# The last store of a row-wise softmax: one DMA of 16 rows per partition, or one of 8 rows and nine DMAs of unequal partition counts for the other 8

## The chip, the cores and the metric

The kernel runs on one core of one Trainium2 chip. The metric is device time in microseconds (us), lower is better. All input comes from the chip's DRAM and all output goes back there, 33.55 MB each way (the page: HBM read 33.55 MB, written 33.55 MB). The profile counts 16 DMA engines, and the semaphore of a store of all rows of a chunk was raised 16 times, here once by each. On the chip the kernel keeps the data in SBUF, in tiles of 128 partitions; a DMA moves rows between SBUF and DRAM. A DMA is issued by an engine's sequencer, and I call it landed when the last of these raises of its semaphore is on record: for the last store of the kernel before, issued at 144.77 us, the first of 16 came at 157.68 and the last at 158.86 us. The profile calls the compute engines DVE (VectorE), ACT (ScalarE), POOL and SP (which here only issues loads); "ACTq" is ACT's instruction sequencer, which issues the stores.

## The reference

```python
def reference(x):                       # x: 16 x 1024 x 512, float32
    x_max = np.max(x, axis=-1, keepdims=True)
    exp_x = np.exp(x - x_max)
    return (exp_x / np.sum(exp_x, axis=-1, keepdims=True)).astype(np.float32)
```

So there are 16384 rows of 512 numbers (2 KB); each row is loaded, normalized and stored once.

## The kernel before

The rows are cut into ten chunks. A chunk of R gives each of the 128 partitions R neighbouring rows, so that one partition's share of a store is one contiguous run of R x 2 KB. Chunks of 16 rows are computed in two groups of 8: DVE takes the maximum, ACT the exponential and the sum, DVE the reciprocal and the scaling. The last group is number 16, rows 8 to 15 of chunk 9. Each load and each store is a single DMA over all 128 partitions.

```python
CHUNKS = [
    (3, 0), (5, 3), (8, 8), (16, 16), (16, 32), (16, 48), (16, 64), (16, 80), (16, 0), (16, 16),
]
GROUP = 8
STORE_ROWS = {3: 8, 4: 8, 5: 8}        # chunks that are stored in two halves of 8 rows
# ... (cut)
        for a, b in zip(cuts, cuts[1:]):
            ends = b == R or b - since >= STORE_ROWS.get(k, R)
            groups.append((k, a, b, since if ends else None))
            since = b if ends else since
# ... (cut)
    def scale(g):
        k, a, b, since = groups[g]
        recip = stats.tile([P, b - a], F32, name="recip", tag="recip")
        nc.vector.reciprocal(out=recip, in_=sums[g])
        for r in range(a, b):
            nc.vector.tensor_scalar_mul(...)          # cut
        if since is not None:
            nc.scalar.dma_start(
                out=dst[k][:, since:b, :], in_=place[k][:, since:b, :]
            )
```

Of the kernel before, what the change touches and what calls it, by code (L numbers as in the profile page):

```python
# [1 line left out]

# [4 lines left out]

F32 = mybir.dt.float32
EXP = mybir.ActivationFunctionType.Exp
AX = mybir.AxisListType.X  # L10


CHUNKS = [
    (3, 0), (5, 3), (8, 8), (16, 16), (16, 32), (16, 48), (16, 64), (16, 80), (16, 0), (16, 16),
]
SBUF_ROWS = 96

EARLY = 8
AFTER_STORE = {2: [8], 3: [9]}

GROUP = 8

FINISH_BEFORE = (1, 2, 3)

STORE_ROWS = {3: 8, 4: 8, 5: 8}

ON_ACT = ()

AT_HEAD = {mybir.EngineType.SP: 1}



def loads_at_the_head(nc):

    main, body = nc.main_func.blocks[0], nc.main_func.blocks[1]
    for engine, count in AT_HEAD.items():
        loads = [
            i
            for i in body.instructions
            if i.engine == engine and type(i).__name__ == "InstDMACopy"  # L40
        ][:count]
        barrier = next(
            n
            for n, i in enumerate(main.instructions)
            if i.engine == engine and type(i).__name__ == "InstDrain"
        )
        for load in loads:
            body.instructions.remove(load)
        main.instructions[barrier:barrier] = loads


@with_exitstack
def kernel(
    ctx: ExitStack,
    tc: tile.TileContext,
    x: bass.AP,
    out: bass.AP,
):
    nc = tc.nc
    nc.at_finalize(loads_at_the_head)  # L60
    P = nc.NUM_PARTITIONS

    x_flat = x.flatten_outer_dims()
    out_flat = out.flatten_outer_dims()
    n, d = x_flat.shape
    assert n == P * sum(R for R, _ in CHUNKS)


    src, dst, at = [], [], 0
    for R, _ in CHUNKS:  # L70
        for flat, views in ((x_flat, src), (out_flat, dst)):
            part = flat[at : at + P * R, :]
            views.append(part.rearrange("(p r) d -> p r d", r=R))
        at += P * R

    data = ctx.enter_context(tc.tile_pool(name="data", bufs=1))
    stats = ctx.enter_context(tc.tile_pool(name="stats", bufs=4))
    held = data.tile([P, SBUF_ROWS, d], F32, name="held")
    place = [held[:, s : s + R, :] for R, s in CHUNKS]


    groups = []
    for k, (R, _) in enumerate(CHUNKS):
        m = max(1, round(R / GROUP))
        cuts = [R * i // m for i in range(m + 1)]
        since = 0
# [4 lines that stand above are left out]
    shift = [None] * len(groups)  # L91
    sums = [None] * len(groups)

    def load(k):
        queue = nc.scalar if k in ON_ACT else nc.sync
        queue.dma_start(out=place[k], in_=src[k])

    def rowmax(g):
        k, a, b, _ = groups[g]
        shift[g] = stats.tile([P, b - a], F32, name="shift", tag="shift")  # L100
        nc.vector.reduce_max(  # L101
            out=shift[g], in_=place[k][:, a:b, :], axis=AX, negate=True
        )

    def exps(g):
        k, a, b, _ = groups[g]
        sums[g] = stats.tile([P, b - a], F32, name="sums", tag="sums")
        for r in range(a, b):
            nc.scalar.activation(  # L109
                out=place[k][:, r, :],  # L110
                in_=place[k][:, r, :],
                func=EXP,
                bias=shift[g][:, r - a : r - a + 1],
                scale=1.0,
                accum_out=sums[g][:, r - a : r - a + 1],
# [7 lines that stand above are left out]
            nc.vector.tensor_scalar_mul(  # L123
                out=place[k][:, r, :],
                in0=place[k][:, r, :],
                scalar1=recip[:, r - a : r - a + 1],
            )
        if since is not None:
            nc.scalar.dma_start(
                out=dst[k][:, since:b, :], in_=place[k][:, since:b, :]  # L130
            )
        if b == CHUNKS[k][0]:
            for later in AFTER_STORE.get(k, ()):
                load(later)

    with tc.manual_schedule():
        for k in range(EARLY):
            load(k)
        waiting = None
        for g, (k, a, _, _) in enumerate(groups):  # L140
            if waiting is not None and a == 0 and k in FINISH_BEFORE:
                scale(waiting)
                waiting = None
            rowmax(g)
            exps(g)
            if waiting is not None:
                scale(waiting)
            waiting = g
        scale(waiting)


# [1 line left out]
_INS = ['x']  # L153
_OUTS = [((16, 1024, 512), 'float32')]


# [23 lines left out]
```

## Time and profile before

| | before |
|---|---|
| time, median of 2 | 162.55 us (162.31 to 162.79) |
| span of the profiled run (that run took 161.52 us) | 159.7 us |
| mean DMA rate over the span | 420 GB/s |
| last store issued, and landed | 144.77 us, 158.86 us |
| last data of the 16 DMA engines | between 157.33 and 158.52 us |

These are lines of the page of the kernel before: the busy time of DVE and ACT, then the busy tenths and the rate of the DMA engines in 40 slices of the span, and the DMA total.

```profile
DVE 123.9 (78%) x162; ACT 93.3 (58%) x257; POOL 0.2 (0%) x4
...
DMA  7999999899999999999999999999999999999993
GB/s 269 433 464 411 389 447 446 383 412 466 402 441 431 460 435 396 439 418 468 427 414 439 414 484 427 396 447 402 435 439 476 418 402 468 443 402 468 427 410 164
DMA packets 3315, 67.13 MB, mean 420 GB/s; under 512 B 368, under 2 KB 368, under 8 KB 624
```

Compute is not the limit: DVE is busy 78% and ACT 58% of the span. The DMA row stands at 9 (90% or more) from the second slice to the next to last. The timeline of the end shows how far compute is ahead. Columns: start, duration, engine, line, operation.

```profile
141.24 0.20 DVE L121 RECIPROCAL recip<-sums 128x8 f32<-128x8 f32 x1 [2.48 <-ACT held L109]
141.48 3.26 DVE L123 TENSOR_SCALAR held<-held,recip 128x512 f32<-128x512 f32 x8
144.77 0.34 ACTq L129 DMA_DIRECT2D out_dram<-held  x1
```

After 144.77 us no engine computes, and yet the kernel lasts 15 us more: the DMA engines work off a queue. The first packets of the store issued at 144.77 start at 147.65 us, when an engine is through with its part of the store ahead. The next lines cut that tail into windows. Columns: window; its length; busy us of DVE, ACT and POOL with instruction counts; granted clock; share of DMA engine time; GB/s. A packet is counted in the window where it starts, so a share can exceed 1.

```profile
150.00:153.00 3.00, 0.00 (x0) 0.00 (x0) 0.00 (x0) 1.00 1.14 492
153.00:156.00 3.00, 0.00 (x0) 0.00 (x0) 0.00 (x0) 1.00 0.83 360
156.00:159.00 3.00, 0.00 (x0) 0.00 (x0) 0.00 (x0) 1.00 0.48 208
159.00:162.00 3.00, 0.00 (x0) 0.00 (x0) 0.00 (x0) 1.00 0.00 0
```

Here share and rate fall together: 492/1.14, 360/0.83 and 208/0.48 are all about 432 GB/s. While a DMA engine is busy, it moves bytes at the same rate in all three windows. In the packet records, each 32 KB packet (one partition's share) of the last store takes 1.213 us (one took 1.226); the 128 packets form 16 rows of eight, back to back, one row for each engine. The engines end within 1.2 us of each other.

### The profile page before, as it was taken

The page shows a single profiled execution, that of the slowest core. Times are in us where ns is not written, and L with a number is a line of the kernel's source. Part 1 is how long each engine was busy: PE and PEld are TensorE (multiplying, and loading weights), DVE is VectorE, ACT ScalarE, POOL GpSimd, SP SyncE. Part 2 cuts the span into 40 slices and gives each one's busy share as a digit, 9 for nine tenths or more (in the row PEclk, how much of TensorE's full clock was granted, in tenths as well). Part 3 has the DMA queues.
Part 4 walks back from the last instruction along what each step waited for, and adds up shares of the span by engine and source line. Part 5 has one row for each costly group of instructions (what it writes and reads, how often), then busy time and mean ns, then how long its engine had stood idle before and what let it go on. Part 6 is the DMA issues. An engine that isn't in the chain of part 4 may idle for free.

```text
span 159.7 us, 521 instructions
## 1 busy us (share of the span) xinstructions
DVE 123.9 (78%) x162; ACT 93.3 (58%) x257; POOL 0.2 (0%) x4
## 2 busy tenths in 40 slices
DVE  0481870799699999999999999999999999762000
ACT  0718129208994959595868677686859595930000
POOL 0000000000000000000000000000000000000000
DMA  7999999899999999999999999999999999999993
GB/s 269 433 464 411 389 447 446 383 412 466 402 441 431 460 435 396 439 418 468 427 414 439 414 484 427 396 447 402 435 439 476 418 402 468 443 402 468 427 410 164
DMA packets 3315, 67.13 MB, mean 420 GB/s; under 512 B 368, under 2 KB 368, under 8 KB 624
## 3 DMA queue, kind: packets, MB, share of 16 engines
q1 hardware_dynamic: 1440, 33.56, 49.5%
q10 hardware_dynamic: 1872, 33.56, 48.9%
q14 instruction: 3, 0.02, 0.0%
HBM read 33.55 MB, written 33.55 MB: 420 GB/s over the span
## 4 chain that ended last, share of the span: by engine, by line
DVE 70%; ACT 14%; issue 3%; DMA 3%; DVEq 0%; ACTq 0%
DVE shift L101 38%; DVE held L123 30%; ACT held L109 14%; DMA held<-in_x_dram 3%; DVE recip L121 2%; DVEq L175 0%; ACTq L109 0%
## 5 line engine op out<-in xcount | busy, mean ns | idle before, releaser
L109 ACT ACTIVATE held<-held,shift 128x512 f32<-128x512 f32 x128 | 90.5, 709 | 43.4 <-DVE shift L101 33.2
L101 DVE TENSOR_REDUCE shift<-held 128x8 f32<-128x4096 f32 (+2 forms) x17 | 70.6, 4161 | 4.5 <-DMA held<-in_x_dram 4.5
L123 DVE TENSOR_SCALAR held<-held,recip 128x512 f32<-128x512 f32 x128 | 52.2, 481 | 0.6
L109 ACT ACTIVATION_READ_ACCUMULATOR held<-held,shift 128x1 f32 x128 | 24.0, 187 | 0.0
L121 DVE RECIPROCAL recip<-sums 128x8 f32<-128x8 f32 (+2 forms) x17 | 3.3, 193 | 15.8 <-ACT held L109 15.8
L109 ACT ACT_TABLE_LOAD x1 | 1.3, 1283 | 4.5 <-DMA held<-in_x_dram 4.5
L164 POOL MEMSET const-bfloat16-1.0<- 128x1 bf16 x1 | 0.1, 102 | 0.0
L164 POOL MEMSET const-uint8-127<- 128x1 uint8 x1 | 0.1, 102 | 0.0
L164 POOL MEMSET const-float32-1.0<- 128x1 f32 x1 | 0.1, 99 | 0.0
L164 POOL MEMSET const-float32-0.0<- 128x1 f32 x1 | 0.1, 98 | 0.2 <-issue 0.2
## 6 DMA issues: line engine op xcount, KB each, us to landing
held<-in_x_dram SPq DMA_DIRECT2D x7, 4096.0 KB, 41.8
out_dram<-held ACTq DMA_DIRECT2D x4, 4096.0 KB, 21.0
out_dram<-held ACTq DMA_DIRECT2D x7, 2048.0 KB, 35.5
held<-in_x_dram SPq DMA_DIRECT2D x1, 2048.0 KB, 11.3
held<-in_x_dram SPq DMA_DIRECT2D x1, 1280.0 KB, 6.7
out_dram<-held ACTq DMA_DIRECT2D x1, 1280.0 KB, 20.0
held<-in_x_dram SPq DMA_DIRECT2D x1, 768.0 KB, 4.5
out_dram<-held ACTq DMA_DIRECT2D x1, 768.0 KB, 15.7
```

The source lines that it names most:

```text
L101: nc.vector.reduce_max(out=shift[g], in_=place[k][:, a:b, :], axis=AX, negate=True)
L109: nc.scalar.activation(out=place[k][:, r, :], in_=place[k][:, r, :], func=EXP, bias=shift[g][:, r - a : r - a + 1], scale=1.0, accum_out=s ...
L121: nc.vector.reciprocal(out=recip, in_=sums[g])
L123: nc.vector.tensor_scalar_mul(out=place[k][:, r, :], in0=place[k][:, r, :], scalar1=recip[:, r - a : r - a + 1],)
L164: nc = _bacc.Bacc("TRN2", target_bir_lowering=False, num_devices=1)
```

## The change

The intent: the first half of chunk 9 is stored as soon as it is ready. The last 8 rows per partition, 16 KB each, are cut into nine DMAs with partition counts that give the 16 DMA engines unequal numbers of packets: in the trace of the change the DMAs of 15, 14, 12, 8, 7, 4, 3 and 1 partitions land 15, 14, 12, 8, 7, 4, 3 and 1 times, that of 64 lands 16 times.

```diff
-STORE_ROWS = {3: 8, 4: 8, 5: 8}
+STORE_ROWS = {3: 8, 4: 8, 5: 8, 9: 8}
+
+SHARES = {16: (64, 15, 14, 12, 8, 7, 4, 3, 1)}
...
         if since is not None:
-            nc.scalar.dma_start(
-                out=dst[k][:, since:b, :], in_=place[k][:, since:b, :]
-            )
+            p = 0
+            for n in SHARES.get(g, (nc.NUM_PARTITIONS,)):
+                nc.scalar.dma_start(
+                    out=dst[k][p : p + n, since:b, :],
+                    in_=place[k][p : p + n, since:b, :],
+                )
+                p += n
```

## The prediction

> **What bounds the kernel now.** The DMA engines. The page's slices show DMA busy 9 tenths from the second to the next to last, mean 420 GB/s for 67.13 MB; DVE is busy 78%, ACT 58%. At the end the queue is deep: in the timeline the last store (4 MB) is issued at 144.77 us, when compute is over, yet it lands only 14.1 us later, at 158.9 (DMA view and landing records). Its first packets start at 147.6, when the store ahead is through. So bytes left per DMA engine set the tail, not the time of issue. In the packet records each engine moves a 32 KB packet every 1.21 us (27.1 GB/s), all 16 back to back, and ends between 157.33 and 158.52; landings spread from 157.68 to 158.86, span 159.74. Perfect balance would gain about 0.6 us (0.4%), no more.
>
> **What the change does.**
> 1. Chunk 9's first 8 rows are stored at about 138.8 instead of 144.8. The queue is full then: worth 0. Bytes are the same, in 16 KB packets (0.605 us each at that rate).
> 2. Nine more DMA issues on ACT, 0.34 us each (timeline), about 3 us, eight of them after ACT's last work; the 12 us of backlog hide them: 0.
> 3. Completion semaphores are reused round robin over eight; an issue waits for the DMA that used its semaphore before (trace: load 5 was issued at 4.47, load 0 had landed at 4.46). By that order the DMA of 4 partitions waits for chunk 8's store (149.2), that of 3 for the first half (about 153), that of 1 for the DMA of 64. Mostly hidden behind engine 0's queue.
> 4. Unequal work. [...] Engine 0 gets 4 x 0.605 = 2.4 us more. If it was an early engine (157.33) it ends at 159.75, if a late one at 160.9: +1.2 to +2.4 us. The staircase overshoots a spread of 1.2 us.
> 5. [...]
>
> **Critical path.** All of 4 and 5 lies on it: nothing follows but the end.
>
> **Prediction.** [...] Point 166.8, range 163.0 to 174.0. Faster by over 2%: 0.02; within 2%: 0.41; slower: 0.57.
>
> **What would show it.** [...]0.61 throughout with one engine's queue outlasting others by up to 4 us (imbalance alone); late issues of the last three DMAs on ACT; the first-half store at 138.8.
>
> **What would make it wrong.** Engine speeds or the assignment of engines differing from step 4, so that the staircase balances something I can't see (then -0.5%); semaphore waits longer than thought.

Unequal work was to add 1.2 to 2.4 us to the 162.55 of before: 163.8 to 165 us. Step 5 was a supposition about packets of partitions that are stored together slowing each other; my model of it had the last data at 166 to 171 us instead of 158.5, +8 to +13 us, and its sign was to be packets of 1.2 us or more. The branch with it was 167 to 175 us and got 55 to 60%. The point, 166.8, lies between the two branches; the range and the three chances cover both.

Step 4 needs only an "engine 0" that is in all nine DMAs: 4 packets of the DMA of 64 and one of each of the other eight, 12 instead of 8. The number is just a name. The trace of the change, below, shows that 12 is the most that an engine can have got; that an engine did get 12 was my estimate. Step 3 agrees with the traces: in those of before and of the change all loads and stores raise the same eight semaphores; in the change the last nine DMAs take them in turn, and that of 1 partition has the semaphore of that of 64 and was issued at 159.44 us, when that had landed at 159.42.

## The result, and the profile after

The median rose from 162.55 to 169.81 us, by 7.26 us. The ratio is 1.0478 (95% interval 1.0398 to 1.0559). Ratios here and below are from the fast runs of both kernels; they are not quite the quotients of the medians that I quote (1.0447 here). Executions over 1.5% slower than the fastest of the same kernel are left out of the means. Later the change ran again, at 168.15 us against 161.56, ratio 1.0405 (1.0355 to 1.0455).

The page after, the lines that answer to those of before:

```profile
DVE 123.9 (74%) x162; ACT 93.3 (56%) x257; POOL 0.2 (0%) x4
...
DMA  7999999999999999999999999999999999999830
GB/s 282 408 429 418 429 445 401 434 450 416 416 425 449 425 435 445 410 421 429 457 414 468 429 410 466 386 433 429 461 421 453 406 468 398 468 386 340 187 117 23
DMA packets 3523, 67.14 MB, mean 400 GB/s; under 512 B 448, under 2 KB 448, under 8 KB 704
```

The busy times of DVE and ACT are the same. Only the last four slices differ. In the slice with 187 GB/s the DMA row still shows an 8 (80 to 90% busy): busy engines, less than half of the bytes. The timeline of the end:

```profile
138.68 0.34 ACTq L133 DMA_DIRECT2D out_dram<-held  x1
...
141.36 3.26 DVE L125 TENSOR_SCALAR held<-held,recip 128x512 f32<-128x512 f32 x8
144.65 15.02 ACTq L133 DMA_DIRECT2D out_dram<-held  x9
```

The first half is issued at 138.68, and compute ends at 144.6 as before. The nine issues spread over 15.02 us. The windows:

```profile
150.00:153.00 3.00, 0.00 (x0) 0.00 (x0) 0.00 (x0) 1.00 1.12 431
153.00:156.00 3.00, 0.00 (x0) 0.00 (x0) 0.00 (x0) 1.00 1.04 235
156.00:159.00 3.00, 0.00 (x0) 0.00 (x0) 0.00 (x0) 1.00 0.93 208
159.00:162.00 3.00, 0.00 (x0) 0.00 (x0) 0.00 (x0) 1.00 0.53 153
162.00:165.00 3.00, 0.00 (x0) 0.00 (x0) 0.00 (x0) 1.00 0.14 49
165.00:168.00 3.00, 0.00 (x0) 0.00 (x0) 0.00 (x0) 1.00 0.06 22
```

The quotient has changed: 235/1.04 = 226 GB/s and 208/0.93 = 224 GB/s per full share, about half of before. After 162 us the share is small: a few engines finish alone.

The packet records say it packet by packet. I take the packets that start after 152.4 us, nearly all of them of the last 2 MB. Of 138 packets of 16 KB, 54 last about the usual 0.611 us and 51 last 1.2 us or more; the mean is 1.044, the longest 2.656. In the run with one DMA of 128 partitions (below) all 134 last 0.611 us.

The landing records tell which DMA ended when. They also tell how many engines each DMA used, as I read them: the semaphores of the DMAs of 15, 14, 12, 8, 7, 4, 3 and 1 partitions show 15, 14, 12, 8, 7, 4, 3 and 1 landings, one for each packet, each DMA with one more early write (of that of 3, for example, at 156.34 us, its landings from 160.71). The DMA of 64 shows 16 landings, so 4 packets for each. With at most one packet from each of the other eight, an engine can have got 12 at most. Which engines they were the counts do not show. The packet records show one engine with 11, its 4 of the DMA of 64 and 7 more: from 155.09 to 160.38 us it took one packet of each of the DMAs of 15, 14, 12, 8, 7, 4 and 3, one right after the other. The last landing of each DMA, with its issue (from the instruction and landing records):

```
partitions   64      15      14      12      8       7       4       3       1
issued    144.65  145.22  146.88  147.92  149.17  150.43  151.69  155.52  159.44
landed    159.42  161.63  164.37  164.98  165.59  166.20  166.81  167.05  162.86
```

Only an engine in all nine DMAs can have 12 packets, and its last is then the DMA of one partition. That landed at 162.86, 4.2 us before the end. So an engine with 12 packets did not bound the kernel. From 164.37 to 166.81 the last landings follow each other at 0.61 us: this looks like one engine that had fallen behind. Its packet in the DMA of 14 took 2.479 us (161.545 to 164.024 in the packet records), and then its four packets in the DMAs of 12, 8, 7 and 4 followed at full speed, 0.611 us each. The very last landing, of the DMA of 3 at 167.05, is another engine's, also with packets of over 1 us shortly before.

### The profile page after: what moved, and what is told of

Same layout as the page of the kernel before. It is cut to its first block, busy times and chain, and to the rows that moved or that the text cites. A ratio compares the mean times of both kernels' runs of the same rounds, so it can differ in the third digit from the quotient of the medians.

```text
span 167.9 us, 531 instructions
## 1 busy us (share of the span) xinstructions
DVE 123.9 (74%) x162; ACT 93.3 (56%) x257; POOL 0.2 (0%) x4
## 4 chain that ended last, share of the span: by engine, by line
DVE 67%; ACT 13%; issue 3%; DMA 3%; DVEq 0%; ACTq 0%
DVE shift L103 37%; DVE held L125 29%; ACT held L111 13%; DMA held<-in_x_dram 3%; DVE recip L123 1%; DVEq L181 0%; ACTq L133 0%; ACTq L111 0%
```

## The experiments

Three theories stand against each other; a fourth, which no run separates from the first, is named with the pair of eight DMAs below.

- **Partitions together.** Packets of different engines slow each other when the DMAs under way take only a part of the partitions, neighbours more than distant ones. This was my supposition, and no record here names what the packets would share; whether the times agree with it is what the runs test.
- **Unequal work.** One engine can get 12 packets (4 + 8 by the landing counts above) instead of 8.
- **Issues and waits.** Nine issues, and the last ones wait for a semaphore that an unfinished DMA still uses (the DMA of 1 was issued at 159.44, when that of 64 had landed at 159.42).

The recorded expectations also held terms for the first theory, from my model of what the packets share. No run shows that model, so these terms are cut from the texts, and so are statements about which engines a DMA uses that came from no trace; what I expected with the cut terms is said beside each.

All outputs are right. Each experiment replaces `SHARES`, or the loop over it by one over pieces with partition step and column range. Medians of before were 161.54 (first group of four), 162.09 (second) and 161.56 us (third). Kernels are compared only within the same rounds.

### One half, one DMA

```diff
-SHARES = {16: (64, 15, 14, 12, 8, 7, 4, 3, 1)}
+SHARES = {16: (128,)}
```

> Undoes the nine shares, keeps the earlier store of the first 8 rows: the last 8 rows go out as one DMA of 128 partitions. All theories that blame the nine shares[...] expect the time of before, 162.5 +- 0.5 us. If splitting chunk 9's store in two (earlier store, 16 KB packets) costs anything itself, it shows here as a part of the +7.3 us.

Measured: 161.85 us, ratio 1.0013 (0.9968 to 1.0057). The earlier store of the first half and the smaller packets cost and gain nothing clear of noise. By the interval all but at most 0.9 us of the loss is in the nine shares.

### Two DMAs of 64

```diff
+SHARES = {16: (64, 64)}
```

> Last 8 rows as two DMAs of 64 partitions: every DMA engine gets 8 packets of 16 KB as before, only two issues, and no semaphore that is still in use. [...] Unequal work: +0. Issue time and semaphore waits: +0.

With the term: +3.2 to +3.9 us, 165.7 to 166.4. Measured: 165.57 us, +4.03, ratio 1.0244 (1.0201 to 1.0287). Every engine has its 8 packets (a DMA of 64 landed 16 times in the trace of the change) and nothing waits for a semaphore (both issues took 1.95 us together), and yet most of the loss is there. The windows of this run:

```profile
150.00:153.00 3.00, 0.00 (x0) 0.00 (x0) 0.00 (x0) 1.00 1.08 431
153.00:156.00 3.00, 0.00 (x0) 0.00 (x0) 0.00 (x0) 1.00 1.06 251
156.00:159.00 3.00, 0.00 (x0) 0.00 (x0) 0.00 (x0) 1.00 0.92 257
```

The rate drops to 251 GB/s at 153 us, as the first DMA of 64 begins, with the engines still busy. The median packet lasts 1.123 us instead of 0.611. Unequal work and waits, which expected nothing here, can't explain these 4 us.

### The same eight DMAs, with neighbouring or distant partitions

This pair holds the number of DMAs, the bytes and, by my count (one packet of each DMA of 16, as one packet for each landing above), the packets per engine equal, and changes which partitions are handled together.

```diff
# neighbours: (first partition, end, step, first element, end)
+PIECES = {16: [(0, 16, 1, 0, 4096), (16, 32, 1, 0, 4096), ..., (112, 128, 1, 0, 4096)]}
# distant
+PIECES = {16: [(0, 128, 8, 0, 4096), (1, 128, 8, 0, 4096), ..., (7, 128, 8, 0, 4096)]}
```

> Last 8 rows as eight DMAs of 16 neighbouring partitions (0..15, 16..31, ...): every engine gets 8 packets of 16 KB, one from each DMA. [...] Unequal work: +0. Issue time and semaphore waits: some 0 to +3 us, and the same as in the run with partitions 8 apart.

> As the run with eight DMAs of 16 neighbouring partitions, but each DMA takes every 8th partition (i, i+8, ..., i+120): same number of issues, bytes, packets and packets per engine; only which partitions are read together differs. [...] Unequal work: +0. Issue time and semaphore waits: the same time as its twin.

With the terms: neighbours +12.9 to +13.5 us, about 175.5; distant +4.4 us, about 167. Measured: neighbours 168.19 us, +6.65, ratio 1.0397 (1.0360 to 1.0434). Distant 164.66 us, +3.12, ratio 1.0185 (1.0150 to 1.0219). The same two windows, first for the neighbours, then for the distant ones:

```profile
153.00:156.00 3.00, 0.00 (x0) 0.00 (x0) 0.00 (x0) 1.00 0.96 202
156.00:159.00 3.00, 0.00 (x0) 0.00 (x0) 0.00 (x0) 1.00 0.96 224
```

```profile
153.00:156.00 3.00, 0.00 (x0) 0.00 (x0) 0.00 (x0) 1.00 1.15 290
156.00:159.00 3.00, 0.00 (x0) 0.00 (x0) 0.00 (x0) 1.00 0.79 251
```

Mean packet times are 1.195 and 0.916 us. So the partitions themselves matter, with 3.5 us between twins: of the three theories only the first expected that. In both, some engines ran out of packets for a while while the last issue was not yet through (it ended at 160.19 and 158.10 us); summed over the packet records this idle time is worth about 0.35 and 0.2 us of all 16 engines (my estimate), not 3.5.

One more thing differs between the twins. In chunk 9 neighbouring partitions are stored 32 KB apart in DRAM, so partitions 8 apart are also stored 256 KB apart. A conflict on the DRAM side is a rival that no run here separates from one on the SBUF side, since partition and address go together in all of them. Only its simplest form, that near addresses conflict, has something against it: the short DMAs of the last experiment below take partitions 4 apart, nearer than 8, and yet from 156 to 159 us the quotient was 355 GB/s per full share there and 318 (251/0.79) in the distant twin.

The sizes were off. The terms were an estimate of mine, from a step model that let the packets share evenly; it said +12.9 and +4.4, and about half of the first came.

### 64 and four times 16

```diff
+SHARES = {16: (64, 16, 16, 16, 16)}
```

> Shares 64, 16, 16, 16, 16: nearly the partitions of the change in nearly its order, but every engine gets exactly 8 packets, and no issue has to wait for a semaphore still in use. [...] Unequal work: +0, 162.5. Semaphore waits: +0.

With the term: +8.3 us, about 170.8, as slow as the change or slower. Measured: 166.49 us, +4.40, ratio 1.0283 (1.0241 to 1.0324). With equal work by the same count and no waits, 4.4 us of the loss remain. The first theory holds in kind; my step model (+8.3) overstates again. The packet records have both short and very long packets (0.611 to 2.395 us, median 0.796): some pass at full speed and others wait long, which the even sharing of my model would not give.

### Nine DMAs, each over 128 partitions

```diff
# seven single rows, and two halves of the last
+PIECES = {16: [(0, 128, 1, 0, 512), ..., (0, 128, 1, 3072, 3584),
+               (0, 128, 1, 3584, 3840), (0, 128, 1, 3840, 4096)]}
```

> Nine DMAs too, but cut along the row: 128 partitions each, 7 of one row (2 KB per partition) and 2 of half a row. Nine issues with the same reuse of semaphores as in the change (the ninth waits for the first), equal work[...]. [...] Issue time and semaphore waits: several us of the +7.3.

The cut sentence had +0 to +1 us for the first two theories. Measured: 162.65 us, ratio 1.0037 (0.9986 to 1.0087), no difference clear of noise. These issues spread out just like those of the change, and the last was issued at 156.19 us:

```profile
142.00 15.06 ACTq L147 DMA_DIRECT2D out_dram<-held  x9
```

So nine issues over 15 us, among them one that waits for the first of the nine, cost 0.56 us here by the medians, and by the upper end of the interval at most 1.4 us. They are not the 7 us. Small DMAs as such are not either: all 896 packets of 2 KB took 0.084 us.

### Unequal work alone

```diff
# 7 rows of all; of the last row 31 partitions (one engine), 96, and 1
+PIECES = {16: [(0, 128, 1, 0, 3584), (0, 31, 1, 3584, 4096),
+               (31, 127, 1, 3584, 4096), (127, 128, 1, 3584, 4096)]}
```

> Unequal work alone: 7 of the last 8 rows as one DMA of 128 partitions; of the last row, 31 partitions as a DMA[...], then 96 and 1. Engine 0 gets 188 KB, the others 124 KB (the change: 192 KB on engine 0). [...] Unequal work, by bytes: +1.1 to +2.3 us, 163.6 to 164.8. If unequal work were the cause of the +7.3 us it would show some 7 us here. [...]

The first theory expects no more than 1.1 to 2.3 us either; the sum stays 163.6 to 164.8. Measured: 164.25 us, +2.16, ratio 1.0132 (1.0089 to 1.0176). The landing records show a single landing, so one engine, for the DMA of 31; it landed at 160.90, the DMA of 1 behind it at 161.55, while 15 of the 16 landings of the DMA of 96 were in by 158.91. The windows show little slowing: the quotients are 428, 375 and 400 GB/s, and 12 of the 128 packets of 2 KB lasted longer than 0.084 us, up to 0.601.

```profile
153.00:156.00 3.00, 0.00 (x0) 0.00 (x0) 0.00 (x0) 1.00 1.01 432
156.00:159.00 3.00, 0.00 (x0) 0.00 (x0) 0.00 (x0) 1.00 0.61 229
159.00:162.00 3.00, 0.00 (x0) 0.00 (x0) 0.00 (x0) 1.00 0.04 16
```

The engine of the DMA of 31 had 188 KB by my count (112 of the first 7 rows, 62 of the DMA of 31, 12 of that of 96, and 2 if the DMA of 1 was its own too). About as many bytes on one engine as the change can put there (at most 12 x 16 = 192 KB) are thus worth about 2.2 us when nothing else is wrong. It is a real cost, of the size foretold, but only about a third of the loss.

### A finer balance, tried as an improvement

```diff
# on the kernel before: 15 rows of all, then the last row as 108 and as 20 partitions
+PIECES = {16: [(0, 128, 1, 0, 7680), (0, 108, 1, 7680, 8192), (108, 128, 1, 7680, 8192)]}
```

> A try at what the change aimed for, on the kernel before: 15 of the last 16 rows as one DMA of 128 partitions, the last row as 108 partitions[...] and 20[...]. Then -0.5 us at best (162.0)[...].

The aim was that the four engines which end last in the profile of before (158.27 to 158.52 us, the first at 157.33) get nothing of the last row. Which engines a DMA of 108 partitions uses I took from no trace. Measured: 163.17 us, +1.08, ratio 1.0067 (1.0027 to 1.0106). It does not gain, it loses a little. In its trace two of the 128 large packets are long (up to 2.175 us instead of 1.138), and the store ahead of it landed 0.65 us later than in the profile of before (149.86 against 149.21). That lag is older than the cut: the second load already landed at 8.85 us, against 7.50 before. So the trace does not show that the cut itself is what cost 1 us. Whether the late engines were the ones left out stays open. No version of mine beats the kernel before.

### The change again, and two shorter lists of shares

```diff
-SHARES = {16: (64, 15, 14, 12, 8, 7, 4, 3, 1)}
+SHARES = {16: (64, 15, 14, 12, 8, 7, 8)}       # one run
+SHARES = {16: (64, 15, 14, 12, 8, 15)}         # the other
```

> The change itself once more, so that the next three stand beside it on one chip: ratio to before 1.045 to 1.053, about 169.8.

> Shares 64, 15, 14, 12, 8, 7, 8: the last three DMAs of the change (4, 3, 1) in one, so the two issues that wait longest for a semaphore in use are gone, and engine 0 has 10 packets instead of 12. Semaphore waits as the cause: most of the +7.3 goes. Unequal work as the cause: 2 of the 4 packets too many go, so half of it. [...]

> Shares 64, 15, 14, 12, 8, 15: no semaphore wait at all, 9 packets at most on an engine instead of 12. Unequal work alone: +0 to +0.6. [...]

With the terms I expected a loss of 5 to 7.5 us to stay in the first, and +4 to +6 us in the second. Measured: the change 168.15 us, ratio 1.0405 (1.0355 to 1.0455), just under what I had expected. With 8 at the end 169.48, ratio 1.0478 (1.0447 to 1.0509). With 15 at the end 168.34, ratio 1.0408 (1.0371 to 1.0444). Neither is faster. The first allows an engine 10 packets at most instead of 12 and drops the two latest issues. The second has at most 9 packets on an engine and no issue that waits for an unfinished DMA. So in the change neither the waits nor the 12 packets that one engine may have lie on what ends last. The second lost 6.8 us, more than I had expected. The packet records of both show the straggler again: a packet that lasts 3.806 us in the first and 3.142 us in the second, and last landings of successive DMAs 0.6 us apart to the end (163.47, 164.08, 164.71, 165.30 in the second).

### The staircase with short DMAs over partitions 4 apart

```diff
# 32 and 32 partitions, then short DMAs that take every 4th partition
+PIECES = {16: [(0, 32, 1, 0, 4096), (96, 128, 1, 0, 4096),
+               (32, 89, 4, 0, 4096),   # 15     (33, 86, 4, ...) 14
+               (34, 79, 4, 0, 4096),   # 12     (35, 64, 4, ...)  8
+               (67, 96, 4, 0, 4096),   #  8     (82, 95, 4, ...)  4
+               (89, 94, 4, 0, 4096),   #  2     (92, 93, 1, ...)  1
+               ]}
```

> The staircase of the change[...], even more DMAs (10) and the same semaphore waits, but the short DMAs take partitions 4 apart[...]. Unequal work or issues as the cause: the time of the change, 169.8 or more. [...]it drops to what the unequal work costs (+2.2, measured with engine 0 alone)[...], +3 to +5 us in all, 165 to 167.

The last sentence is what the first theory expected; its sum of +3 to +5 us holds, above the measured +2.2, a term for the first two DMAs. Measured: the four runs scatter, 165.30, 166.89, 168.33 and 168.72 us; the last two are slow. The two fast ones give a ratio of 1.0276 (1.0218 to 1.0335), against 1.0405 for the change beside it. The mean of all four, 167.31, is only 0.75 us below the mean of the change's four, 168.06. So the time alone is no proof. The profiled run, the fastest, shows shorter packets: 93 of 140 last about 0.611 us (57 of 138 in the change beside it), the mean is 0.760 (1.058). Its windows, then those of the change:

```profile
153.00:156.00 3.00, 0.00 (x0) 0.00 (x0) 0.00 (x0) 1.00 0.97 306
156.00:159.00 3.00, 0.00 (x0) 0.00 (x0) 0.00 (x0) 1.00 0.77 273
159.00:162.00 3.00, 0.00 (x0) 0.00 (x0) 0.00 (x0) 1.00 0.28 104
```

```profile
153.00:156.00 3.00, 0.00 (x0) 0.00 (x0) 0.00 (x0) 1.00 1.07 257
156.00:159.00 3.00, 0.00 (x0) 0.00 (x0) 0.00 (x0) 1.00 1.00 186
159.00:162.00 3.00, 0.00 (x0) 0.00 (x0) 0.00 (x0) 1.00 0.53 153
```

The quotient is better, most so in the second window (355 against 186 GB/s per full share), where the short DMAs run. What made the other three runs slower is open; they have no trace. In the profiled one the very last DMA was issued at 158.70 us, when the DMA that used its semaphore had landed, and landed itself at 162.29, last of all. So here a wait may bound the end, as it did not in the change.

### The runs together

Added time is the difference of the medians. Packet times are those of the 16 KB packets that start after 152.4 us in the profiled run.

```
last 8 rows as                       added us   packet us: mean, longest   most packets that an engine can have
128                                    +0.31        0.611   0.611                8
8 x 16, partitions 8 apart             +3.12        0.916   1.509                8
64, 64                                 +4.03        1.005   1.709                8
64, 16, 16, 16, 16                     +4.40        0.990   2.395                8
8 x 16, neighbours                     +6.65        1.195   3.204                8
64, 15, 14, 12, 8, 15                  +6.78        1.053   3.142                9
64, 15, 14, 12, 8, 7, 4, 3, 1          +6.59        1.058   3.591               12
64, 15, 14, 12, 8, 7, 8                +7.92        1.094   3.806               10
```

The last column counts as above: the packets of the large DMA and one of each short one. It does not order these times. The longest packet nearly does, but the first trace of the change does not fit: its longest was 2.656 us at +7.26. The last experiment is left out because its runs scatter; its profiled run, 3.74 us above the median of before, had a mean of 0.760 and a longest of 2.112.

## Why the prediction was right or wrong

The prediction was right: slower by over 2%, 169.81 us within 163.0 to 174.0, in the upper branch (167 to 175) that had been given 55 to 60%. The point 166.8 lay between the branches and is 3 us low because of that.

1. *DMA bound, and the earlier store is worth 0:* right. With the split alone the ratio was 1.0013.
2. *Nine issues of 0.34 us, hidden:* the consequence was right, the size was not. Issues took 0.54 to 2.21 us, the last one 0.23, and with their waits spread over 15.02 us. The nine DMAs over 128 partitions did the same and lost 0.4% (interval -0.1% to +0.9%).
3. *Waits for reused semaphores, mostly hidden:* right for the change. The DMA of 1 was issued when that of 64 had landed (159.44 after 159.42), and that of 3 when the first half had (155.52 after 155.50, where about 153 was foretold). Dropping all waits gained nothing (168.34 against 168.15).
4. *Unequal work, +1.2 to +2.4 us:* the size was right for that cost alone, +2.16 measured. But that the engine with 12 packets ends last failed: if there was one, it ended 4.2 us before the end, and a list with 9 packets at most is as slow. The two costs do not add.
5. *The step, +8 to +13 us, last data at 166 to 171 us:* right in kind (in DMAs over a part of the partitions packets took 1.044 us in the mean instead of 0.611), too large in size. The last data came at 166.71 us in the first trace, just inside, and at 164.52 in the second, outside; the loss was 7.26 and 6.59 us. Where work was equal the model was further off: my even sharing gave +12.9 and +8.3 us where +6.65 and +4.40 were measured. That the time itself came out in the range is in part luck: the range spanned both branches, and the overstated term was partly made up by some 2 us of the unequal lists, whose reason is open (below). The records show uneven times instead: single packets last up to 3.8 us, six times 0.61, beside others that pass in 0.61.

What is shown: with equal work, two or five issues and no unfinished semaphore, DMAs over a part of the partitions still cost 4.0 to 4.4 us, and of two lists of eight that differ in the distance of the partitions (and with it of the DRAM addresses) one costs 3.5 us more. What it is that the packets share is not shown. No record names it, and a conflict on the DRAM side was not tested.

What is open: why the unequal lists lose 2.2 to 3.5 us more than 64 and four times 16, although unequal work as such is not what ends last. In three of the four traces of such lists the records show one engine that is held up by a packet of 2.5 to 3.8 us and then runs its rest alone; in the second trace of the change several engines end within 0.3 us of the last. Why that one, and whether the unequal counts bring it about, no run here tells.

## What to carry to other kernels

A DMA over a part of the partitions ran at half speed here though the engines were busy (226 instead of 432 GB/s per full share), so the share of busy time must be read beside the GB/s: their quotient tells. To split a store like this one, split along the row and keep all 128 partitions in each DMA; nine such pieces cost nothing clear of noise here (+0.4%, at most 0.9%). Before balancing DMA engines, read how far apart they end: 1.2 us of spread can't repay a cut over partitions that cost 3.1 to 6.7 us here even with equal work.

## Two more things that the traces show

- An issue from ACT took 0.34 us alone (the one at 138.68 us in the change), but most of those that directly followed another took 1.0 to 1.6 us (five of the nine in the change; with 128 partitions five in a row took 1.2, and after a pause the next two 0.34 again). A long queue in front is not enough: the last store of before had 14 us of it and took 0.34. The reason is open.
- One DMA engine fell behind early in some executions, as I read the landings, and stayed so: in the trace of the change the slowest landing of the second load is at 8.77 us with the next at 7.58, and the same gap is there at 150.65 against 149.27. The traces of 64 and four times 16 (150.73 against 149.20) and of the nine DMAs over 128 partitions (150.60 against 149.37) have such a gap too. The trace of the kernel before (7.50 and 7.48) and the second of the change (149.26 and 149.18) have none, and the loss is there all the same (+6.59). Differences of about a microsecond between executions of one kernel may come from this; no run tests it.
